# First adaLN modulation of a hybrid decoder layer: features on the partitions, one multiply-and-sum per column

## The chip, the cores and the metric

The kernel runs on one core of a Trainium2 chip. The metric is the device time of one execution in microseconds, as the median of several runs. The core has five engines with a queue each: TensorE (PE, whose weight loads are shown as PEld), VectorE (DVE), ScalarE (ACT), GpSimd (POOL) and SyncE (SP), which only issues transfers. Every queue is worked through in its own order, and semaphores tie the queues together.

## The reference, cut to what matters

One decoder layer on x of 512 tokens by 1024 features, with a conditioning vector c of 1024 numbers:

```
c_act = silu(c)
mod = c_act @ w_ada + b_ada                       # 1024 x 6144, all float32
sh1, sc1, g1, sh2, sc2, g2 = split(mod, 6)
h = rmsnorm(x, gain0) * (1 + sc1) + sh1
proj = h @ w_in                                   # queries, keys, values of both head groups
x = x + g1 * rmsnorm(attention(proj) @ w_out, gain1)
h = rmsnorm(x, gain2) * (1 + sc2) + sh2
x = x + g2 * rmsnorm(square(relu(h @ w1 + b1)) @ w2 + b2, gain3)
```

The change concerns how sh1 and sc1 (2048 of the 6144 numbers of mod) are computed, and what stands around that.

## The kernel before

Every large product is made in three float32r passes: a matrix is split into a high part (ACT, a copy) and a low part (the rest, by DVE or POOL), and the passes are high by high, high by low and low by high. Features are cut into eight chunks of 128 (KC), tokens into four tiles of 128 (NT).

The first stage goes from the start to the end of six products (q and k of three pairs of heads), which gather in six of the eight PSUM banks (qk_ps). It loops over the chunks kc. For each chunk, `w0_split` makes the high and the low part of the input weights (ACT, then two POOL instructions), `chunk_in` transposes x of this chunk on PE into a PSUM bank, applies the modulation on ACT twice (once rounded into hh, once in place) and takes the difference on DVE into hl. PE then runs 18 products of 128 by 512: six with w0hi and hh, six with w0lo and hh, six with w0hi and hl. The modulation of a chunk needs two columns for its 128 features, sh1 and sc1, with features on the partitions.

These columns are sums of 1024 terms. Before the change, a weight tile has 128 of the 1024 inputs on the partitions, and `acc0` and `ada_acc` add eight such slices, each scaled by one number of silu(c) for each partition (two on ACT, six on DVE, in two accumulators, which DVE adds). `ada_sums` then sums over the partitions on PE with a column of ones and leaves the result in PSUM, and `ada_cols` adds the bias and makes (1 + sc1) times the gain. Chunks 0 and 1 are made alone, chunks 2 to 7 in pairs (`groups`).

The order of every engine in the first stage is written out by hand (`tc.manual_schedule`): an instruction waits behind those that the program names before it on its engine. In the chunk loop the counter k tells at which of the 18 products something is issued. The sums of a pair stand in the PE queue at k = 2 of odd chunks, the transposes of the next chunk at k = 6 or 8. All large loads are issued by SP, in the order of the program; the weight tiles of the modulation rotate through 12 buffers. Nine bfloat16 products of zeros (`heat`) stand ahead of the first transposes. After the first stage, the order of ACT, DVE, POOL and SP is a planner's, which works from its own estimates, while PE's order stays written out by hand; near the end everything is by hand again.

The rows of x are normalised first: `square` on ACT gives the sums of squares into s2 (half of the last tile on DVE), `rstd` adds on DVE and takes the power on POOL, `scale_x` multiplies.

What follows the stage: `ws.make` splits three blocks of the value weights behind chunks 5, 6 and 7 (ACT, then DVE at L85); three further blocks reuse their raw buffers, and SP issues those loads, then others, then the first bias strips (L602), which are read from vec_1, a small table that the kernel computes and stores in DRAM at its start. DVE adds the strips to the scores at L649. The other four parts of mod are made later by `ada_wide` on DVE, on the way through attention.

## Time and profile before

| | us |
|---|---|
| median of 3 runs | 622.37 |
| lowest, highest | 621.87, 622.49 |
| profiled execution | 623.07 |
| its span, first to last instruction | 621.3 |
| PE busy in the span | 580.3 |
| DVE busy | 315.2 |
| ACT busy | 279.2 |
| POOL busy | 321.6 |

The span is what the trace covers; the 1.8 us between it and the execution's time lie outside of the first and the last instruction. Busy time is a sum over the span and says nothing about which engine ends last in a stretch.

### The profile page before, as it was taken

What the parts mean: (1) busy time and instruction counts of PE and PEld (TensorE: products, weight loads), DVE (VectorE), ACT (ScalarE), POOL (GpSimd) and SP (SyncE); (2) the same over time, 40 slices, a digit from 0 to 9 for tenths busy, and PEclk for the clock granted to TensorE, in tenths of its full rate; (3) what the DMA queues carried; (4) which work ended last, traced back from release to release, by engine and by line L of the source; (5) the groups of instructions that cost most, each with busy time, mean ns of one, the idle gap of its engine ahead of it and who ended that gap; (6) DMA issues with size and microseconds to landing.
All of it is one profiled execution on the core that took longest, in us unless ns stands there. A gap on an engine that the chain in (4) does not pass through costs nothing.

```text
span 621.3 us, 8137 instructions
## 1 busy us (share of the span) xinstructions
PE 580.3 (93%) x2829; PEld 482.0 (78%) x2829; DVE 315.2 (51%) x599; ACT 279.2 (45%) x532; POOL 321.6 (52%) x333
## 2 busy tenths in 40 slices
PE   2789989999897999999999999999999999999994
PEld 0477889887675888898888888788888888888883
DVE  4646679999998756535255555522401111111037
ACT  4624776578667545773233332233522333323122
POOL 1514234666898653636555555655544444446432
PEclk9969999999998999999999999999999999999998
DMA  8990569686466207734244432223232233333105
GB/s 308 419 383 1 189 129 260 128 170 224 140 185 207 84 1 270 236 106 149 89 136 136 146 125 99 80 93 101 71 112 89 100 103 102 102 101 116 56 17 186
DMA packets 29677, 89.31 MB, mean 144 GB/s; under 512 B 3427, under 2 KB 7587, under 8 KB 29636
## 3 DMA queue, kind: packets, MB, share of 16 engines
q1 hardware_dynamic: 28816, 86.52, 43.5%
q10 hardware_dynamic: 692, 2.23, 0.9%
q8 instruction: 22, 0.36, 0.3%
q14 instruction: 19, 0.16, 0.1%
q0 software_dynamic: 128, 0.05, 0.1%
HBM read 84.56 MB, written 4.22 MB: 143 GB/s over the span
## 4 chain that ended last, share of the span: by engine, by line
PE 55%; DVE 2%; ACT 2%; DMA 1%; issue 1%; POOL 0%; DVEq 0%; POOLq 0%; ACTq 0%; SPq 0%
PE u L97 9%; PE u L98 9%; PE u L96 9%; PE y L98 9%; PE y L97 9%; PE y L96 9%; DVE zg L1090 1%; ACT hf L379 1%; DMA x<-in_x 1%; ACT h2h L378 0%; DVE x L933 0%; DMA out_x<-zg 0%; ACT sq L208 0%; PE adarow L299 0%; POOL zg L1087 0%
## 5 line engine op out<-in xcount | busy, mean ns | idle before, releaser
L85 POOL TENSOR_TENSOR wlo<-raw,whi 128x512 fp32r<-128x512 f32 (+1 forms) x140 | 192.4, 1393 | 157.7 <-ACT whi L83 157.2
L83 ACT ACTIVATE whi<-raw 128x1024 fp32r<-128x1024 f32 (+5 forms) x87 | 80.7, 934 | 130.8 <-PE u L97 108.9
L97 PE MATMUL u<-h2l,whi 128*128 128x512 f32 (+1 forms) x280 | 104.2, 372 | 1.2 <-POOL h2l L380 1.1
L96 PE MATMUL u<-h2h,whi 128*128 128x512 f32 (+1 forms) x280 | 104.7, 374 | 0.0
L98 PE MATMUL u<-h2h,wlo 128*128 128x512 f32 (+1 forms) x280 | 103.8, 371 | 0.0
L97 PE MATMUL y<-wlo,ring_h2h 128*128 128x512 f32 x232 | 90.2, 389 | 0.0
L98 PE MATMUL y<-whi,ring_h2l 128*128 128x512 f32 x232 | 90.2, 389 | 0.0
L96 PE MATMUL y<-whi,ring_h2h 128*128 128x512 f32 x232 | 90.1, 389 | 0.0
L284 DVE SCALAR_TENSOR_TENSOR adaacc<-adar,c_act,adaacc 128x512 f32<-128x512 f32 x56 | 66.7, 1191 | 0.0
L97 PEld LDWEIGHTS u<-h2l,whi 128*128 128x128 f32 x280 | 52.7, 188 | 11.3 <-POOL h2l L380 1.7
L96 PEld LDWEIGHTS u<-h2h,whi 128*128 128x128 f32 x280 | 52.7, 188 | 9.2 <-ACT whi L83 0.2
L98 PEld LDWEIGHTS u<-h2h,wlo 128*128 128x128 f32 x280 | 52.7, 188 | 9.2
L663 POOL TENSOR_SCALAR w<-w,st 128x128 f32<-128x128 f32 (+2 forms) x64 | 38.2, 599 | 38.2 <-DVE st L662 32.8
L97 PEld LDWEIGHTS y<-wlo,ring_h2h 128*128 128x128 f32 x232 | 43.5, 188 | 9.1
L96 PEld LDWEIGHTS y<-whi,ring_h2h 128*128 128x128 f32 x232 | 43.5, 188 | 9.0
L98 PEld LDWEIGHTS y<-whi,ring_h2l 128*128 128x128 f32 x232 | 43.5, 188 | 9.0
L656 ACT ACTIVATE w<-w,st 128x128 f32<-128x128 f32 (+3 forms) x64 | 33.4, 522 | 28.2 <-DVE st L649 26.1
L85 POOL TENSOR_TENSOR w0lo<-w0raw,w0hi 128x384 fp32r<-128x384 f32 x16 | 17.2, 1095 | 29.3 <-ACT w0hi L83 29.3
L672 PE MATMUL p<-ident,w 128*128 128x128 f32 x136 | 25.9, 279 | 6.4 <-POOL w L663 5.9
L672 PEld LDWEIGHTS p<-ident,w 128*128 128x128 f32 x136 | 17.3, 142 | 13.4 <-POOL w L663 9.6
L686 ACT ACTIVATE pth<-p 128x384 fp32r<-128x384 f32 (+3 forms) x48 | 22.2, 466 | 10.1 <-PE p L672 9.6
L687 DVE TENSOR_TENSOR ptl<-p,pth 128x384 fp32r<-128x384 f32 (+3 forms) x48 | 25.0, 523 | 0.8 <-ACT pth L686 0.6
(222 smaller groups left out, 1093.9 us busy)
## 6 DMA issues: line engine op xcount, KB each, us to landing
raw<-in_w SPq DMA_DIRECT2D x63, 512.0 KB, 3.3
adar<-in_ada_r SPq DMA_DIRECT2D x32, 512.0 KB, 4.1
ada<-in_ada_c SPq DMA_DIRECT2D x16, 512.0 KB, 8.6
woraw<-in_w_out SPq DMA_DIRECT2D x8, 512.0 KB, 4.4
raw<-in_w_in SPq DMA_DIRECT2D x7, 512.0 KB, 6.7
w0raw<-in_w_in SPq DMA_DIRECT2D x8, 384.0 KB, 9.1
strip<-vec SPq DMA_DIRECT2D x24, 128.0 KB, 4.1
xn<-in_x SPq DMA_DIRECT2D x4, 512.0 KB, 10.0
```

What stands on the lines that cost most here:

```text
L83: nc.scalar.activation(hi[:, a:b], src[:, a:b], AF.Copy)
L85: return eng.tensor_sub(lo[:, a:b], src[:, a:b], f32(hi[:, a:b])).ins
L96: nc.tensor.matmul(ps, lh, rh, start=start, stop=False, **kw)
L97: nc.tensor.matmul(ps, lh, rl, start=False, stop=False, **kw)
L98: nc.tensor.matmul(ps, ll, rh, start=False, stop=stop, **kw)
L284: nc.vector.scalar_tensor_tensor(a, w, c_act[:, j:j + 1], a, op0=ALU.mult, op1=ALU.add)
L379: nc.scalar.activation(hf[:, :n], tp, AF.Identity, bias=sh_col, scale=a_col)
L656: anchor["act"] = nc.scalar.activation(w[:, :m], w[:, :m], AF.Exp, bias=st[:, 0:1], scale=-1.0, accum_out=st[:, 1:2]).ins
L663: nc.gpsimd.tensor_scalar(w[:, :n], w[:, :n], st[:, 2:3], 1.0, op0=ALU.mult, op1=ALU.mult)
L672: nc.tensor.transpose(p_ps[:, (c0 + j) * P:(c0 + j + 1) * P], self.w[i][:, j * P:(j + 1) * P], ident)
L686: nc.scalar.activation(dst(self.pth), src, AF.Copy)
L687: nc.vector.tensor_sub(dst(self.ptl), src, f32(dst(self.pth)))
```

## The change

Each partition now holds one output feature, and the 1024 inputs lie on the free axis: a weight tile is 128 features by 1024 inputs, two tiles (sh1, sc1) for each chunk. silu(c) is spread over all partitions once (eight products with the identity on PE, two copies on ACT into c_bc). A column is then one DVE instruction that multiplies tile and c_bc and sums along the free axis (`ada_dot`); chunk 0 is made in halves of 512. The pass over the partitions on PE, the ACT scalings and the accumulators go. Columns are made chunk by chunk, two chunks ahead of their use, and not in pairs. The input to `ada_cols` lies in SBUF (sums0) instead of PSUM. Loads follow use: chunk 0's tiles, x, then for each chunk its input weights and the next chunk's tiles. `chunk_in` is cut into `hi_in` and `lo_in`, with DVE's two sums around `lo_in`. The clearing of s2 comes after chunk 0's columns in DVE's queue, the two copies into vec_sb come behind the first `square` on ACT, the store of vec_1 goes from ACT's queue to SP's, and there are eight heat products instead of nine, in the PE queue behind the spreading of c and the two vec products, with no sums ahead of them.

```diff
-    groups = [(0,), (1,), (2, 3), (4, 5), (6, 7)]
+    ada_raws = [[] for _ in range(KC)]
+    def ada_load(kc):
+        for b in range(2):
...
-    ada_load(0, 2)
-    ada_load(1, 2)
+    ada_load(0)
     for i in range(NT):
         nc.sync.dma_start(out=xn[i], in_=x[i * P:(i + 1) * P, :])
+    for kc in range(1, KC):
+        w0_load(kc - 1)
+        ada_load(kc)
+    w0_load(KC - 1)
...
+    c_bc = first.tile([P, DM], F32, name="c_bc")
+    for h in range(2):
+        ps = bank(f"cbc{h}")
+        for j in range(4):
+            nc.tensor.matmul(ps[:, j * P:(j + 1) * P], c_act[:, 4 * h + j:4 * h + j + 1].to_broadcast([P, P]), ident,
+                             start=True, stop=True)
+        nc.scalar.activation(c_bc[:, h * 512:h * 512 + 512], ps, AF.Copy)
...
-    nc.scalar.dma_start(out=vec_1.rearrange("q h n -> h q n"), in_=vec_sb)
...
+    def ada_dot(kc, b, cs, acc):
+        junk = first.tile([P, 1024], F32, tag="dot", name=f"dot{kc}_{b}_{cs.start}", bufs=1)
+        nc.vector.scalar_tensor_tensor(junk[:, cs], ada_raws[kc][b][:, cs], 1.0, c_bc[:, cs], op0=ALU.mult,
+                                       op1=ALU.mult, accum_out=acc)
+    def dot(kc, b):
+        ada_dot(kc, b, slice(0, 1024), sums0[:, kc, b:b + 1])
+    def cols(kc):
+        ada_cols(0, [kc], sums0[:, kc, :])
...
-    pairs = [(g, next(g)) for g in (acc0(0), acc0(1))]
+    for h in range(2):
+        for b in range(2):
+            ada_dot(0, b, slice(h * 512, h * 512 + 512), parts0[:, h, b:b + 1])
+    nc.vector.tensor_add(sums0[:, 0, :], parts0[:, 0, :], parts0[:, 1, :])
+    cols(0)
     nc.vector.memset(s2[:, :, 0:2], 0.0)
     for i in range(NT):
...
         square(junk[:, :n], xn[i][:, :n], s2[:, i, 0:1])
+        if i == 0:
+            for q, ps in enumerate(vec_ps):
+                nc.scalar.activation(vec_sb[:, q, :], ps[0:8, :NVEC], AF.Copy)
+            nc.sync.dma_start(out=vec_1.rearrange("q h n -> h q n"), in_=vec_sb)
-    for j in range(9):
+    for j in range(8):
         nc.tensor.matmul(cold, heat[:, 0:P], heat, start=True, stop=True)
...
     w0_split(0)
-    chunk_in(0)
-    for i in range(NT):
-        scale_x(i, 1, act=i >= 2)
-    g = acc0(2)
-    acc = next(g)
+    hi_in(0)
+    scale_x(0, 1)
+    scale_x(1, 1)
+    scale_x(2, 1, act=True)
+    scale_x(3, 1, act=True)
+    dot(1, 0)
+    dot(1, 1)
+    lo_in(0)
+    cols(1)
...
         for k in range(18):
+            if nxt < KC and k == (8 if kc else 11):
+                hi_in(nxt)
+                if nxt + 1 < KC:
+                    dot(nxt + 1, 0)
+                lo_in(nxt)
+                if nxt + 1 < KC:
+                    dot(nxt + 1, 1)
+                    cols(nxt + 1)
```

## Rows read from the trace of the kernel before

**Rows 1.** The page: busy time of every engine over the span.
```profile
PE 580.3 (93%) x2829; PEld 482.0 (78%) x2829; DVE 315.2 (51%) x599; ACT 279.2 (45%) x532; POOL 321.6 (52%) x333
```

**Rows 2.** Windows: stretch, its length, busy time of each engine, PEclk, DMA, GB/s.
```profile
28.00:34.00 6.00, 0.85 (x5) 0.80 (x4) 5.71 (x7) 1.87 (x3) 2.71 (x3) 0.71 1.02 413
34.00:41.00 7.00, 7.00 (x23) 5.79 (x23) 2.64 (x7) 1.42 (x2) 0.00 (x0) 0.51 1.03 420
72.00:100.00 28.00, 25.29 (x172) 24.28 (x170) 23.49 (x56) 20.45 (x49) 10.40 (x14) 1.00 0.79 216
100.00:200.00 100.00, 91.41 (x514) 76.11 (x513) 96.31 (x247) 72.31 (x182) 71.49 (x97) 0.99 0.66 177
200.00:500.00 300.00, 298.79 (x1435) 249.88 (x1434) 128.88 (x177) 119.99 (x204) 160.33 (x146) 0.99 0.36 119
```

**Rows 3.** Timeline of PE at 33 us: start, duration, instruction, count, idle before.
```profile
33.23 1.84 PE L249 MATMUL adaps<-ones,acc 128*128 128x1 f32 x8 [5.15 <-DVE acc L322]
34.93 2.05 PE L436 MATMUL qk<-hh,w0hi 128*128 128x512 f32 x4
```

**Rows 4.** Timeline of DVE in the same stretch.
```profile
27.54 0.69 DVE L396 TENSOR_TENSOR hl<-tp,hh 128x512 fp32r<-128x512 f32 x1 [1.23 <-ACT tp L395]
28.15 4.21 DVE L228 SCALAR_TENSOR_TENSOR acc<-ada,c_act,acc 128x512 f32<-128x512 f32 x4
```

**Rows 5.** Timeline of PE: first products of chunks 6 and 7.
```profile
63.47 1.53 PE L436 MATMUL qk<-hh,w0hi 128*128 128x512 f32 x6
...
68.05 1.52 PE L436 MATMUL qk<-hh,w0hi 128*128 128x512 f32 x6
```

**Rows 6.** Timeline of the start, all engines, up to the first product.
```profile
3.89 0.17 DVE L204 TENSOR_TENSOR c_act<-c_sb,ce 128x8 f32<-128x8 f32 x1
...
5.59 2.72 PE L310 MATMUL vec<-oneh,rel_sb 33*8 33x384 f32 x4 [5.59 <-DMA rel_sb<-in_rel]
...
11.84 1.06 ACT L208 ACTIVATE sqx<-xn 128x1024 f32<-128x1024 f32 x1 [0.88 <-DMA xn<-in_x]
...
15.60 0.63 ACT L208 ACTIVATE sqx<-xn 128x512 f32<-128x512 f32 x1 [0.15 <-DMA xn<-in_x]
...
16.48 3.98 PE L350 MATMUL cold<-heat 128*128 128x512 bf16 x9
...
18.54 0.68 DVE L357 SCALAR_TENSOR_TENSOR sqy<-xn 128x512 f32<-128x512 f32 x1
...
19.58 0.56 POOL L213 TENSOR_TENSOR s2x<-s2x,mhalf 128x1 f32<-128x1 f32 x1 [0.76 <-DVE s2x L212]
...
20.94 0.78 ACT L394 ACTIVATE hh<-tp,mods 128x512 fp32r<-128x512 f32 x1 [3.63 <-PE tp L371]
...
21.77 1.66 PE L436 MATMUL qk<-hh,w0hi 128*128 128x512 f32 x6 [0.87 <-ACT hh L394]
```

**Rows 7.** Timeline of PE: four transposes at the low clock.
```profile
37.64 1.05 PE L371 MATMUL tp<-ident,xn 128*128 128x128 f32 x4
```

**Rows 8.** Timeline of DVE and POOL, narrow stretches where both read SBUF.
```profile
28.72 1.03 POOL L85 TENSOR_TENSOR w0lo<-w0raw,w0hi 128x384 fp32r<-128x384 f32 x1 [0.44 <-ACT w0hi L83]
28.81 1.49 DVE L228 SCALAR_TENSOR_TENSOR acc<-ada,c_act,acc 128x512 f32<-128x512 f32 x1
...
48.66 1.47 POOL L85 TENSOR_TENSOR w0lo<-w0raw,w0hi 128x384 fp32r<-128x384 f32 x1
49.18 0.15 DVE L256 TENSOR_TENSOR mods<-adaps,bada_c 128x4 f32<-128x4 f32 x1
49.37 0.21 DVE L259 TENSOR_SCALAR mods<-mods,gain_c 128x1 f32<-128x1 f32 x1
```

**Rows 9.** Timeline behind the stage: SP's issues and DVE.
```profile
72.89 0.97 SPq L602 DMA_DIRECT2D strip<-vec  x1
...
67.85 1.89 DVE L85 TENSOR_TENSOR wlo<-raw,whi 128x960 fp32r<-128x960 f32 x2 [0.23 <-ACT whi L83]
...
81.38 0.29 DVE L649 CUSTOM_DVE_ANT_0 w<-s,strip 128x128 f32<-128x128 f32 x1 [2.96 <-DMA strip<-vec]
```

More of the change, by code (lines that the diff above doesn't have):

```diff
@@ L217, in halves, with ada_sums @@
         return [t[:, 0:512], t[:, 512:1024]]
-    def ada_acc(accs, raws, per, begin):
-        n = 1024 // per
-        for b, raw in enumerate(raws):
-            for j in range(per):
-                if b * per + j >= begin:
-                    w = raw[:, j * n:(j + 1) * n]
-                    cj = c_act[:, b * per + j:b * per + j + 1]
-                    nc.vector.scalar_tensor_tensor(accs[j % 2], w, cj, accs[j % 2], op0=ALU.mult, op1=ALU.add)
-                    yield
     mods = const.tile([P, 2, KC, 3], F32, name="mods")
-    def ada_sums(layer, kcs, acc, wait=lambda: None):
+    def ada_sums(layer, kcs, acc):
         n = 2 * len(kcs)
-        if layer:
-            sums = small.tile([P, n], F32, tag=f"sums{n}", name=f"sums{layer}_{kcs[0]}")
-            for h in range(0, n, 4):
-                m = min(4, n - h)
-                ps = bank(f"adaps{layer}_{kcs[0]}_{h}")
-                for s in range(m):
-                    nc.tensor.transpose(ps[:, s * P:(s + 1) * P], acc[:, (h + s) * P:(h + s + 1) * P], ident)
-                wait()
-                nc.vector.tensor_reduce(out=sums[:, h:h + m], in_=ps[:, :m * P].rearrange("p (s q) -> p s q", q=P),
-                                        op=ALU.add, axis=mybir.AxisListType.X)
-            return sums
-        ps = bank(f"adaps{layer}_{kcs[0]}")
-        for s in range(n):
-            nc.tensor.matmul(ps[:, s:s + 1], acc[:, s * P:(s + 1) * P], ones[:, 0:1], start=True, stop=True)
-        return ps
+        sums = small.tile([P, n], F32, tag=f"sums{n}", name=f"sums{layer}_{kcs[0]}")
+        for h in range(0, n, 4):
+            m = min(4, n - h)
+            ps = bank(f"adaps{layer}_{kcs[0]}_{h}")
+            for s in range(m):
+                nc.tensor.transpose(ps[:, s * P:(s + 1) * P], acc[:, (h + s) * P:(h + s + 1) * P], ident)
+            nc.vector.tensor_reduce(out=sums[:, h:h + m], in_=ps[:, :m * P].rearrange("p (s q) -> p s q", q=P),
+                                    op=ALU.add, axis=mybir.AxisListType.X)
+        return sums
     def ada_cols(layer, kcs, ps):
@@ L395, in chunk_in, with lo_in @@
         nc.scalar.activation(tp, tp, AF.Identity, bias=sh_col, scale=a_col)
-        nc.vector.tensor_sub(hl[:, kc, :], tp, f32(hh[:, kc, :]))
+    def lo_in(kc):
+        nc.vector.tensor_sub(hl[:, kc, :], tps[kc], f32(hh[:, kc, :]))
+    tps = {}
     w0_split(0)
-    chunk_in(0)
-    for i in range(NT):
-        scale_x(i, 1, act=i >= 2)
-    g = acc0(2)
-    acc = next(g)
-    def some(n):
-        for _ in range(n):
-            next(g, None)
+    hi_in(0)
[7 more added lines that the diff above has]
+    cols(1)
     for kc in range(KC):
@@ L1125, in _lay_out @@
     unit = lambda m: m.transpose(1, 0, 2).reshape(P, -1)
[L1126 removed]
+    wt = a["w_ada"][0].reshape(DM, 2, 3, KC, P)[:, 0, 0:2]
+    o["ada_c"] = c(wt.transpose(3, 2, 1, 0).reshape(P, KC * 2 * DM))
     o["ada_r"] = c(np.stack([unit(m) for m in (w[:, :, 0, 2], cols(1, range(4)), cols(1, range(4, 8)), w[:, :, 1, 2])]))
```

66 lines of the change are left out of this document (9 added, 57 removed).

## The prediction

> **What bounds the kernel now.** The page comes first. PE is busy for 580.3 of 621.3 us [rows 1], so whatever shortens the run must take idle time, or slow time, out of PE's queue. The windows say where that time lies. From 200 to 500 us PE idles 1.2 us in all, and nothing can be won there [rows 2]. From 72 to 200 us DVE is the fuller engine (23.5 of 28 us, then 96.3 of 100) and PE idles 2.7 and 8.6 us. From 28 to 34 us PE works 0.85 of 6 us; from 34 to 41 us it is busy all the time, but at a granted clock of 0.51, the lower of its two levels (1.2 instead of 2.4 GHz).
>
> The timeline explains the hole. PE waits 5.15 us, until 33.23, for the accumulator of chunks 2 and 3 [rows 3]. DVE is late with it: after the hl of chunk 1 at 27.54 come four scaled sums, which take 4.21 us, and the addition [rows 4]. The partition sums of that pair stand in PE's queue ahead of 16 products of chunk 1. After the idle stretch the clock is low, and it is back at full level by 41 [rows 2]. So the first stage is set by DVE's queue, and then by the clock.
>
> What a chunk costs when nothing is late: from the first product of chunk 6 to that of chunk 7 it is 68.05 - 63.47 = 4.58 us, 18 products and four transposes [rows 5], so about 0.222 us for a product and 0.56 us for the transposes. The first product starts at 21.77 [rows 6]. Eight such chunks, the last without transposes, would be 36.1 us and end at 57.9. The stage ends at 72.2 (68.05 plus 18 products and the last one's tail). Some 14 us are there to be won, and not more.
>
> **The start.** Before, the chain is x, squares, power, scaling, transposes, hh, first product. The first square waits for x until 11.84, the last until 15.60 [rows 6]. Two of the eight 512 KB loads ahead of the end of x now come later: at the 413 GB/s of this stretch [rows 2] that is 1.05 MB or 2.5 us, so x lands from about 9.3 to 13.1. But the clearing of s2 now stands behind chunk 0's columns on DVE, and the squares write into s2. How late is that?
>
> silu(c) is ready at 4.06 [rows 6], and I let PE begin at 4.2. The eight spreading products are two passes each, as two vec products show as x4 [rows 6]. Each pass loads 128 columns and streams 128. No row has this form. The nearest is a float32 transpose at the low clock: 1.05 / 4 = 0.26 us [rows 7]. The bound above is load and stream one after the other: 0.26 plus what 128 of vec's 384 columns take (2.72 / 4 / 3 = 0.23 [rows 6]), 0.49. I take 0.26, as the same load and stream stand in that row: 16 passes are 4.2 us, the two halves end at 6.3 and 8.4, and ACT copies them in some 0.6 each. DVE's four halves are of the form of L357, 0.68 us for 512 columns with the sum [rows 6], 0.72 with the hand-over: 7.0 to 8.4 and 9.1 to 10.5. Additions and clearing end at 11.05. The squares then run 11.1 to 16.6, with vec_sb's two copies (about 0.5 each) among them, against 11.84 to 16.3 before. The earlier x is thus mostly given away. The last power comes at 17.2, not 19.58, since DVE's half square and additions stand free now; scaling, transposes, and hh (0.78) put the first product at 19.2, 2.6 us earlier. With serial passes it would be 22.9.
>
> **The clock at the start.** The heat products lie behind vec and need nothing else, so PE runs them at about 11 to 13.4 and then has four transposes until 19.2. Before, they ran from 16.48, right up to the transposes [rows 6]. An idle stretch like this one cost the high level at 31 us, and it came back some 6 us after the products began at 34.93 [rows 2, 3]. I take the same here: products at twice 0.222 for 6 us, a loss of 3.0 us (bounds: 0 if the level holds, 3.0 or more otherwise). Chunk 0 then ends at 26.9.
>
> **The chunks.** PE loses the partition sums and ACT the scalings; neither was last at full pace, so I count nothing for them beyond the waits. DVE's work for a chunk: two sums over 1024. From 256 to 512 columns such an instruction grows by 0.0010 us a column as the rows of L228 have it (0.74 for 512), so 0.68 + 0.53 = 1.21, 1.24 with the hand-over. With hl (0.66 to the next) and the two small ones (0.15 and 0.21 [rows 8]) that is 3.5 us, below PE's 4.58. But POOL makes w0lo, twice 1.0 us a chunk, and the two engines take turns: DVE's sum begun at 28.81 takes 1.49 instead of 0.74, as POOL works until 29.7 [rows 8]. 3.5 + 2.0 is 5.5 at worst, 3.5 at best.
>
> The Trainium skill, "SBUF — State Buffer", section "SBUF: two separate sides", says why: VectorE with two SBUF inputs and GpSimd hold a shared port pair in turn, each for its whole instruction. Rows 8 agree. The same rule speaks against a detail of this change: L256 read its sums from PSUM and took 0.15 us during a POOL instruction that had 48.66 to 50.13 [rows 8]; now both its inputs lie in SBUF, and it would wait. By the rule the stage ends at 61.4, without it for L256 at 58.2.
>
> What decides is a loop that closes once a chunk. hh needs the columns, the second ACT pass follows hh, hl follows that, on DVE the second sum of the next-but-one chunk stands behind hl, and the columns behind that: 0.75 + 0.68 + 0.66 + 1.24 + 0.37 and four hand-overs of 0.05 are 3.9 us. If L256 waits for one POOL instruction of 1.0, it is 4.9; when another falls before the sum, 5.9. I laid out the queues of PE, ACT, DVE and POOL by these durations: chunks 1 and 2 go at PE's pace (end 36.0), chunks 3 to 7 take 4.7 to 5.9, 5.1 on the mean: 36.0 + 25.4 = 61.4. I take the waiting L256, since other two-input sums wait. That is 10.8 us before 72.2.
>
> Weights of the modulation are not late: chunk 7's land after some 13 MB, 13 / 0.413 = 32 us and the start, near 37, and are used at 52. Their buffers are freed by chunk 1's sums at 22.4, before SP comes to them.
>
> **Behind the stage.** Not all 10.8 us arrive. The third value block's split (DVE, L85) ended at 69.74, 2.5 us before the stage; in my layout DVE's queue puts it behind the last columns and hl, at 61.5. SP's third reload waits for it, the strips queue behind, and the first bias sum waited 2.96 us for its strip until 81.38 [rows 9], ahead of a stretch in which DVE is the bound. That start moves by 69.74 - 61.5 = 8.2 us. I count 8.5, a little PE gain included. vec_1's store costs SP one issue, hidden by strips that are read 40 us later. 623.07 - 8.5 = 614.6 for the profiled execution, 0.7 above the median, so 613.9.
>
> **Rivals.** (a) As worked out: 612 to 617, chance 0.52. (b) L256 doesn't wait and PE sets the pace: the stage ends at 58.2, the splits 12 us earlier: 610.4. For it: DVE has 1 us of slack a chunk; against: rows 8. 0.18. (c) The spreading passes are serial: first product at 22.9, 3.7 us later, stage end at 65.1, 3.7 us less gain: 617.6. 0.12. (d) The other side: the clock stays low. A chunk at the low level is 18 x 0.444 + 4 x 0.26 = 9.0 us, 4.4 more than 4.58. Low through chunk 3 it takes back what was won; low for 40 us, the stage ends at 74.8 and the run at 625. For it: the long gap ahead of the first product; against: from 34.93 on it rose under the same kind of products [rows 2, 3]. 0.05. (e) The change gives nothing: the long sum costs 2.2 us instead of 1.24, DVE needs 6.9 us a chunk, the stage ends at 72.1: 622. Against: L357 is the same form. 0.05. (f) The planner lays the order from 72 to 200 us otherwise. DVE has under 9 us of slack in 128, so some us go either way; only a loss of 8.5 would turn the sign. 0.08.
>
> **How the numbers follow.** The forecast is (a). 608.5 to 620 takes in (b), (c), and most of (f), and leaves out (d), (e) and the far ends, under 0.2. Differences below 0.2% (1.2 us) can't be told from no change. Faster: (a), (b), (c), most of (f) and a little of (e), 0.89. Same: rest of (e) and some of (f), 0.03. Slower: (d) and the remainder, 0.08.
>
> **What would show it.** First product near 19 us; clock at 0.5 in its first 6 us; no PE idle above 2 us from there on; hh waiting for L259 from chunk 3; L256 near 1 us after the second sum's end in chunks with POOL at work; last product of the stage near 61; first L649 near 73. The prediction is wrong if the stage ends above 66, or if it ends near 61 and the first 100:200 DVE stretch eats the gain.

## The result, and the profile after

| | before | after |
|---|---|---|
| median, same chip (us) | 622.12 | 608.24 |
| lowest, highest | 621.68, 622.49 | 607.16, 608.40 |
| ratio of the times, 95% interval | | 0.9773, [0.9756, 0.9790] |
| profiled execution, its span | 623.07, 621.3 | 608.38, 606.6 |

The change makes the kernel 13.9 us faster. The forecast was 613.9, with a range down to 608.5: the sign was right, the gain was larger than forecast, and the time lies 0.3 us below the range. One execution of the first experiment, in which every product ran at half pace, is left out of its times.

The page of the kernel after, busy time of each engine [rows 1]:

```profile
PE 573.3 (95%) x2812; PEld 478.0 (79%) x2812; DVE 322.0 (53%) x604; ACT 274.5 (45%) x524; POOL 327.1 (54%) x333
```

DVE and POOL are busy for longer than before. PE is busy for 7.0 us less and idle for 7.7 us less (33.3 instead of 41.0), with almost as many instructions: the kernel won less by doing less work than by losing less time, in waits and at the low clock. The windows of the kernel after, same stretches and columns as [rows 2]:

```profile
28.00:34.00 6.00, 6.00 (x30) 4.92 (x29) 5.93 (x9) 3.36 (x5) 3.67 (x3) 1.00 1.03 404
34.00:41.00 7.00, 7.00 (x36) 5.77 (x35) 6.93 (x12) 3.34 (x5) 4.12 (x3) 1.00 1.03 409
72.00:100.00 28.00, 26.35 (x172) 24.49 (x173) 27.87 (x80) 21.35 (x60) 13.87 (x18) 1.00 0.79 179
100.00:200.00 100.00, 90.72 (x503) 75.21 (x502) 93.47 (x242) 68.88 (x170) 76.01 (x109) 0.98 0.62 175
200.00:500.00 300.00, 298.77 (x1420) 249.39 (x1419) 119.29 (x145) 116.17 (x190) 158.48 (x132) 1.00 0.34 117
```

The hole of 28 to 34 us is gone, and with it the low clock of 34 to 41 (1.00, was 0.51). What is new is DVE's column: 5.93 of 6 and 6.93 of 7 us, with PE full as well. The two engines run level, and neither has slack.

The start, from the timelines of PE, DVE and ACT of the kernel after [rows 6]:

```profile
4.37 3.76 PE L284 MATMUL cbc<-ident,c_act 128*128 128x128 f32 x16 [4.37 <-DVE c_act L197]
...
10.81 0.07 DVE L326 MEMSET s2x<- 128x8 f32 x1
...
10.91 1.06 ACT L201 ACTIVATE sqx<-xn 128x1024 f32<-128x1024 f32 x1 [2.16 <-DVE s2x L326]
...
9.52 1.90 PE L336 MATMUL cold<-heat 128*128 128x512 bf16 x8
18.66 2.92 PE L411 MATMUL qk<-hh,w0hi 128*128 128x512 f32 x6 [0.87 <-ACT hh L378]
```

The first square waits 2.16 us for the clearing of s2, as forecast. The first six products take 2.92 us, against 1.52 at full pace. The granted clock says so too; windows of the kernel after:

```profile
16.00:18.00 2.00, 0.95 (x2) 0.36 (x2) 1.46 (x6) 0.68 (x2) 1.62 (x3) 0.50 1.04 412
...
20.00:22.00 2.00, 2.00 (x6) 1.51 (x6) 1.97 (x3) 1.86 (x3) 0.06 (x1) 0.52 1.04 414
22.00:24.00 2.00, 2.00 (x13) 1.66 (x12) 1.96 (x6) 0.43 (x1) 2.00 (x2) 1.00 1.03 408
```

The chunks, from PE's timeline of the kernel after (first products of chunks 1, 2, 6 and 7 [rows 5]):

```profile
24.84 1.53 PE L411 MATMUL qk<-hh,w0hi 128*128 128x512 f32 x6
29.43 1.52 PE L411 MATMUL qk<-hh,w0hi 128*128 128x512 f32 x6
...
47.76 1.66 PE L411 MATMUL qk<-hh,w0hi 128*128 128x512 f32 x6
54.23 1.65 PE L411 MATMUL qk<-hh,w0hi 128*128 128x512 f32 x6 [1.62 <-ACT hh L378]
```

Chunks 1 to 5 take 4.54 to 4.66 us each, PE's own pace. Only chunk 7 starts late, by one hole of 1.62 us, and the next timeline, DVE's, shows where it comes from: two instructions of the wide modulation (L257, L259), placed there by the planner, stand ahead of chunk 7's column addition (L231).

```profile
48.55 0.48 DVE L257 TENSOR_SCALAR adaacc<-adar,c_act 128x512 f32<-128x512 f32 x1
48.95 0.68 DVE L382 TENSOR_TENSOR hl<-tp,hh 128x512 fp32r<-128x512 f32 x1
49.55 1.21 DVE L302 SCALAR_TENSOR_TENSOR dot<-ada,c_bc 128x1024 f32<-128x1024 f32 x1
...
50.69 1.49 DVE L259 SCALAR_TENSOR_TENSOR adaacc<-adar,c_act,adaacc 128x512 f32<-128x512 f32 x1
52.11 0.95 DVE L231 TENSOR_TENSOR mods<-sums,bada_c 128x2 f32<-128x2 f32 x1
```

One ordinary cycle on DVE, earlier in the same timeline [rows 4, 8]:

```profile
29.85 0.68 DVE L382 TENSOR_TENSOR hl<-tp,hh 128x512 fp32r<-128x512 f32 x1
30.45 1.21 DVE L302 SCALAR_TENSOR_TENSOR dot<-ada,c_bc 128x1024 f32<-128x1024 f32 x1
...
31.71 0.85 DVE L231 TENSOR_TENSOR mods<-sums,bada_c 128x2 f32<-128x2 f32 x1
...
32.72 1.88 DVE L302 SCALAR_TENSOR_TENSOR dot<-ada,c_bc 128x1024 f32<-128x1024 f32 x1
...
34.53 0.68 DVE L382 TENSOR_TENSOR hl<-tp,hh 128x512 fp32r<-128x512 f32 x1
```

From hl (29.85) to hl (34.53) it is 4.68 us, without idle time: 0.1 us more than PE's 4.57. DVE falls behind by that much a chunk, and chunk 5 is the first that takes longer on PE, 4.66.

Behind the stage, from the timelines of DVE and SP [rows 9]: the third split ends at 57.68, the strip is issued at 61.54, and the first bias sum starts at 68.74.

```profile
55.78 1.90 DVE L85 TENSOR_TENSOR wlo<-raw,whi 128x960 fp32r<-128x960 f32 x2 [0.23 <-ACT whi L83]
...
61.54 0.46 SPq L577 DMA_DIRECT2D strip<-vec  x1
...
65.82 0.69 DVE L503 SCALAR_TENSOR_TENSOR q<-qk,q 64x512 fp32r<-64x512 f32 x1 [0.62 <-ACT q L502]
68.74 0.29 DVE L624 CUSTOM_DVE_ANT_0 w<-s,strip 128x128 f32<-128x128 f32 x1 [2.22 <-PE s L617]
```

The releaser in the last row is to be doubted: that score product had begun at 65.54 and takes 0.28 us. The engine that it names had long been done.

Seven marks, read from the timelines of either kernel (us; a chunk's or a stretch's first instruction, but the split's end):

```
                         before   after   earlier by
first product             21.77   18.66     3.11
stage end (first v)       72.12   58.45    13.67
third split, end          69.74   57.68    12.06
first bias sum            81.38   68.74    12.64
first out-projection y   189.61  175.81    13.80
first u                  256.83  242.16    14.67
end of span              621.3   606.6     14.7
```

By PE's timelines, the 13.67 us at the stage's end come from these places. The first product gives 3.11. Chunk 1, with the hole and most of the low clock behind it, gives 9.82 (14.41 us before, 4.59 after). Chunks 3 and 5, in which the sums of the other two pairs stood, give 3.25 together (6.24 and 6.23 before, 4.56 and 4.66 after). Chunk 0 takes back 0.49 (5.69 before, 6.18 after), and chunk 6 with the hole behind it 1.89 (4.58 before, 6.47 after).

### The profile page after: what moved, and what is told of

It is laid out like the page before. It is cut to its first block, busy times and chain, and to the rows that moved or that the text cites. A ratio compares the mean times of both kernels' runs of the same rounds, so it can differ in the third digit from the quotient of the medians.

```text
span 606.6 us, 8099 instructions
## 1 busy us (share of the span) xinstructions
PE 573.3 (95%) x2812; PEld 478.0 (79%) x2812; DVE 322.0 (53%) x604; ACT 274.5 (45%) x524; POOL 327.1 (54%) x333
## 4 chain that ended last, share of the span: by engine, by line
PE 56%; DVE 2%; ACT 2%; DMA 1%; issue 1%; POOL 0%; DVEq 0%; POOLq 0%; ACTq 0%; SPq 0%
PE u L97 10%; PE u L98 9%; PE u L96 9%; PE y L97 9%; PE y L98 9%; PE y L96 9%; DVE zg L1065 1%; DMA x<-in_x 1%; ACT hf L363 1%; ACT h2h L362 0%; DVE x L908 0%; DMA out_x<-zg 0%; ACT sq L201 0%; PE adarow L274 0%; POOL zg L1062 0%
## 5 line engine op out<-in xcount | busy, mean ns | idle before, releaser
L259 DVE SCALAR_TENSOR_TENSOR adaacc<-adar,c_act,adaacc 128x512 f32<-128x512 f32 x56 | 65.8, 1175 | 0.0
L85 POOL TENSOR_TENSOR w0lo<-w0raw,w0hi 128x384 fp32r<-128x384 f32 x16 | 22.1, 1402 | 13.8 <-ACT w0hi L83 13.8
L1002 DVE TENSOR_TENSOR ring_h2l<-rsq_hl,ring_h2h 128x512 fp32r<-128x512 f32 x8 | 5.5, 694 | 38.0 <-ACT ring_h2h L1001 38.0
```

Source lines behind the costliest of these rows:

```text
L85: return eng.tensor_sub(lo[:, a:b], src[:, a:b], f32(hi[:, a:b])).ins
L259: nc.vector.scalar_tensor_tensor(a, w, c_act[:, j:j + 1], a, op0=ALU.mult, op1=ALU.add)
```

## The experiments

Their order is that in which they were run; a table of their marks stands at the end. Each edit is against the kernel after, if nothing else is said.

**The clearing of s2 ahead of chunk 0's columns.**

```diff
+    nc.vector.memset(s2[:, :, 0:2], 0.0)
     for h in range(2):
         for b in range(2):
             ada_dot(0, b, slice(h * 512, h * 512 + 512), parts0[:, h, b:b + 1])
...
-    nc.vector.memset(s2[:, :, 0:2], 0.0)
```

> Only the clearing of s2 moves ahead of chunk 0's sums in DVE's queue. In the changed kernel the first square idles 2.16 us until that clearing, at 10.91. If the clearing is what the start waits for, the first square begins near 9.2 (x landed, ACT's second copy into c_bc done at 8.8), the first product near 17.0 instead of 18.66, and the run gains 1.5 to 2 us. If x's landing or the copies of vec_sb set the start, nothing moves (under 0.5 us).

606.36 us, ratio 0.9746 [0.9720, 0.9773]. The time alone does not separate it from the kernel after, whose interval overlaps. The start does, read in the run further below that has this edit and one more: there the first square starts at 9.10 instead of 10.91, waiting for x and no longer for the clearing, and the first product at 16.84 instead of 18.66. It is the clearing that does it: with the other edit alone the first square still waits for the clearing, until 11.02, and the first product comes at 18.76.

**Zero products that keep the clock.** Twenty at the start instead of eight, and fourteen between and behind the first four transposes.

```diff
-    for j in range(8):
+    for j in range(20):
         nc.tensor.matmul(cold, heat[:, 0:P], heat, start=True, stop=True)
...
+            for j in range(warm[i]):    # (4, 4, 2, 4) in chunk 0
+                nc.tensor.matmul(qk_ps[0], heat[:, 0:P], heat, start=True, stop=True)
```

> Heat products go from 8 to 20 behind vec, and 4, 4, 2, 4 more behind the four first transposes, so that PE works up to the first product. In the changed kernel the granted clock falls at 15 and the first six products take 0.44 us each. If the idle stretch from 11.4 to 14.3 is the cause, the clock stays at the high level through 22 us, the first six products take 0.22, and chunk 0 goes from 6.2 to about 4.9 us; gain 1.3 us of stage. The rival is that chunk 1's columns (ready at 23.4) hold chunk 1 anyway: then PE waits for hh of chunk 1 and the gain is under 0.5.

609.70 us, ratio 0.9799 [0.9768, 0.9830]: nothing won. PE's timeline of this kernel, chunk 0:

```profile
18.27 1.66 PE L413 MATMUL qk<-hh,w0hi 128*128 128x512 f32 x6
...
22.78 1.66 PE L413 MATMUL qk<-hl,w0hi 128*128 128x512 f32 x6 [1.02 <-DVE hl L384]
```

The six products take 1.66 instead of 2.92 us: the clock was kept. But then PE waits 1.02 us for hl, which stands behind chunk 1's column sums in DVE's queue (it starts at 22.04), and the next chunk starts only 0.57 us earlier than in the kernel after. Full clock moves the wait to DVE.

**The wide modulation not before the last split**, so that it cannot stand ahead of chunk 7's columns.

```diff
+    anchor["dve"] = ws.last_lo
```

> The planner's two early adaacc instructions (0.48 and 1.49 us, in DVE's queue ahead of chunk 7's columns in the changed kernel) are kept behind the last instruction of the stage; nothing else is asked for, but the planner's order behind the stage may differ. If they make the 1.6 us hole of PE ahead of chunk 7, the hole goes and the stage ends near 56.8 instead of 58.5; the run gains 1 to 2 us unless the order behind the stage takes it back. If the hole comes from POOL's turn alone it stays above 1 us.

608.52 us, ratio 0.9772 [0.9742, 0.9802]: no change in the time. The hole is gone (chunk 7 starts at 52.38, the stage ends at 56.58, 1.87 us earlier), which shows the cause of the hole; but the first out-projection product comes at 176.17, 0.36 later than in the kernel after. The first bias sum comes 1.33 us earlier, and the stretch from there to the out-projection takes 1.69 us longer, with the planner's order on DVE changed (see the next section). What the rest of the loss is, no run shows.

**A column addition with one input from SBUF.**

```diff
-        nc.vector.tensor_add(m[:, :, 0:2], ps[:, 0:2 * n].rearrange("p (k s) -> p k s", s=2),
-                             bada_c[:, layer, kcs[0]:kcs[0] + n, :])
+            for s in range(2):
+                nc.vector.tensor_scalar(m[:, 0, s:s + 1], ps[:, s:s + 1], bada_c[:, 0, kcs[0], s:s + 1], 1.0,
+                                        op0=ALU.add, op1=ALU.mult)
```

> The addition of L231 (0.85 us in the changed kernel, two SBUF inputs) becomes two one-input instructions with the bias as a per-partition scalar. By the prediction's layout the wait of this addition is worth 3 us of the stage. By the trace of the changed kernel PE already sets the pace (4.57 us a chunk, against 4.58 at best), so the columns come 0.4 to 0.6 us earlier, the next sum waits that much longer for POOL instead, and the stage gains under 0.5 us.

607.38 us, ratio 0.9765 [0.9738, 0.9792]. DVE's timeline of this kernel:

```profile
30.95 0.33 DVE L233 TENSOR_SCALAR mods<-sums,bada_c 128x1 f32<-128x1 f32 x2
...
31.44 1.53 DVE L307 SCALAR_TENSOR_TENSOR dot<-ada,c_bc 128x1024 f32<-128x1024 f32 x1
```

Two instructions that read one SBUF tensor and a pointer take 0.33 us where one that read two took 0.85: the addition had waited for POOL. DVE now has slack, chunks 1 to 6 go at 4.55 to 4.56 us, chunk 7 starts at 52.12 without a hole and the stage ends at 56.20. The two adaacc instructions still stand ahead of chunk 7's last columns in DVE's queue, and the chunks in between are hardly faster. So the waiting addition had its part in the hole (which takes both it and the adaacc instructions) and hardly any in the pace.

**Chunk 1's weight tiles ahead of x again.**

```diff
     ada_load(0)
+    ada_load(1)
     for i in range(NT):
         nc.sync.dma_start(out=xn[i], in_=x[i * P:(i + 1) * P, :])
     for kc in range(1, KC):
         w0_load(kc - 1)
-        ada_load(kc)
+        if kc > 1:
+            ada_load(kc)
```

> The changed kernel with chunk 1's weight tiles loaded ahead of x again, as before the change. If the load order matters only through x at the start, x lands 2.5 us later, the first square starts near 11.8 instead of 10.9, and the run loses 0.5 to 1.5 us. If the order of loads is a main part of the gain, 4 us or more are lost.

610.63 us, ratio 0.9824 [0.9782, 0.9867]. The first square starts at 11.51 instead of 10.91, the first product at 19.26 (0.60 later), the stage ends at 59.07 (0.62 later). The new order of the loads is worth about 0.6 us where it acts, since in the kernel after the squares wait for the clearing anyway; the time does not tell the two apart, as the intervals overlap.

**Half as long sums for chunks 2 to 7.** The columns of these chunks are sums over 512 of the 1024 inputs; the rest is left out.

```diff
-        ada_dot(kc, b, slice(0, 1024), sums0[:, kc, b:b + 1])
+        ada_dot(kc, b, slice(0, 1024 if kc < 2 else 512), sums0[:, kc, b:b + 1])
```

> The sums of chunks 2 to 7 run over 512 of the 1024 inputs (the other half is left out), 1.1 us less DVE work a chunk. If PE sets the pace of the chunks already, chunks 1 to 5 stay at 4.57 us, only the hole ahead of chunk 7 shrinks, and the run gains 0.5 to 2 us. If DVE's loop sets the pace as the prediction had it, the stage gains 0.5 us or more in each of chunks 3 to 7 beyond that, 3 us in all.

605.21 us, ratio 0.9732 [0.9684, 0.9780]. With half the work in the sums the chunks still take 4.55 us each: PE sets the pace. The stage ends at 55.82, 2.63 us earlier, of which 1.62 is the hole.

**One more sum a chunk** (512 columns, its result unused).

```diff
                 if nxt + 1 < KC:
                     dot(nxt + 1, 1)
+                    ada_dot(nxt + 1, 1, slice(0, 512), parts0[:, 0, 0:1])
```

> For each of chunks 2 to 7 one more sum over 512 columns (0.7 us, its result unused) stands in DVE's queue behind the second sum. In the changed kernel DVE works 6.93 of 7 us in the stage and needs about 4.67 us a chunk. If DVE is level with PE, a chunk now takes 5.3 us or a little more, the stage ends 4 to 5 us later and the run loses 3 to 5. If DVE had the slack of 1 us a chunk that the plain durations give, under 1 us is lost.

617.29 us, ratio 0.9927 [0.9904, 0.9951]. The timelines of PE and DVE of this kernel:

```profile
30.56 1.64 PE L412 MATMUL qk<-hh,w0hi 128*128 128x512 f32 x6 [0.58 <-ACT hh L378]
...
36.49 1.65 PE L412 MATMUL qk<-hh,w0hi 128*128 128x512 f32 x6 [1.11 <-ACT hh L378]
...
37.12 0.69 DVE L382 TENSOR_TENSOR hl<-tp,hh 128x512 fp32r<-128x512 f32 x1 [0.41 <-ACT tp L379]
...
38.98 1.38 DVE L302 SCALAR_TENSOR_TENSOR dot<-ada,c_bc 128x512 f32<-128x512 f32 x1
```

From here a chunk takes 5.93 us (36.49 - 30.56), 1.36 more than in the kernel after, the stage ends 6.5 us later and the run loses 9, more than the 4 to 5 and 3 to 5 expected. The sum of 0.69 us takes 1.38 beside POOL, and DVE now idles 0.41 us a cycle for ACT's second pass, which itself waits for the columns: the loop of the prediction closes. More work on DVE costs at once, and more than its own duration; less work gains nothing in the pace. So DVE stood at the edge.

**The kernel before, with its sums later in PE's queue.** In chunk 1 the partition sums stand at k = 14 and the transposes at k = 16 instead of 2 and 8.

```diff
-                if k == 2:
+                if k == (14 if kc == 1 else 2):
...
-                elif k == 8:
+                elif k == (16 if kc == 1 else 8):
```

> The kernel before, with only the place of the partition sums of chunks 2 and 3 in PE's queue moved from the third to the fifteenth product of chunk 1 (and the transposes of chunk 2 from the ninth to the seventeenth). If the 5.15 us wait there and the low clock after it are the main part of the 14 us, PE works on until about 31, the clock stays at the high level, and the run gains 5 to 7 us. If DVE's lateness is only met again at chunk 2, it gains under 2 us.

619.58 us, ratio to the kernel before 0.9972 [0.9948, 0.9995]. PE's timeline of this kernel, the sums of the three pairs [rows 3] and the first products of chunk 2:

```profile
33.18 1.02 PE L249 MATMUL adaps<-ones,acc 128*128 128x1 f32 x8 [2.46 <-DVE acc L322]
...
36.08 2.77 PE L436 MATMUL qk<-hh,w0hi 128*128 128x512 f32 x6
...
43.00 1.02 PE L249 MATMUL adaps<-ones,acc 128*128 128x1 f32 x8 [0.49 <-DVE acc L322]
...
54.33 1.02 PE L249 MATMUL adaps<-ones,acc 128*128 128x1 f32 x8 [1.03 <-DVE acc L322]
```

DVE's accumulator comes as late as before. PE does other work in the meantime, but still waits 2.46 us instead of 5.15, and the clock falls behind that wait too: six products take 2.77 us. The second pair waits as before (0.49, was 0.51), the third longer (1.03, was 0.52), again with the low clock behind it (0.50 from 56 to 58 us). This placing gives 2.5 us of span, where 5 to 7 were expected; whether another would give more was not tried.

**No low splits for chunks 2 to 7**, so that POOL does not work beside DVE.

```diff
+        if kc < 2:
             split_to(*w0[kc], w0_raw[kc])
+        else:
+            w0[kc][1] = w0[0][1]
+            nc.scalar.activation(w0[kc][0], w0_raw[kc], AF.Copy)
```

> The low parts of the input weights are made for chunks 0 and 1 only; chunks 2 to 7 use chunk 0's low part again (this leaves out twelve POOL instructions of 1.0 us, so q and k lack their right low parts). Nothing else changes. Theory 1 (from chunk 2 on, DVE's column sums of 1.87 us and the column addition of 0.85 us hold 0.66 and 0.69 us of waiting for POOL; DVE's cycle of 4.67 us stands level with PE's 4.57): the first sum of a chunk falls to about 1.21 us, the addition to 0.16 to 0.2, DVE's share of 34 to 41 us from 99% to about 70%, the chunks stay at 4.55 us because PE sets them, and the hole of 1.62 us ahead of chunk 7 goes or shrinks below 0.4; the stage ends near 56.2 instead of 58.45, the run is 1 to 2 us faster than 608.2. Rival (the prediction's picture, in which POOL costs DVE so much that DVE sets the pace): chunks fall by 0.5 us each, the stage ends near 55 or below. Rival (POOL plays no part; 1.87 is what such a sum costs when the array of TensorE is at work): sums stay at 1.87, nothing changes.

606.23 us, ratio 0.9746 [0.9706, 0.9786]. DVE's timeline of this kernel:

```profile
34.42 1.22 DVE L302 SCALAR_TENSOR_TENSOR dot<-ada,c_bc 128x1024 f32<-128x1024 f32 x1
...
35.68 0.16 DVE L231 TENSOR_TENSOR mods<-sums,bada_c 128x2 f32<-128x2 f32 x1
...
38.36 0.69 DVE L387 TENSOR_TENSOR hl<-tp,hh 128x512 fp32r<-128x512 f32 x1 [1.13 <-ACT tp L384]
```

1.88 and 0.85 us fall to 1.22 and 0.16: 1.35 us of every cycle on DVE was waiting for POOL. DVE is now idle 1.13 us a cycle, and the chunks take 4.55 to 4.57 as before. The hole is gone, the stage ends 1.7 us earlier.

**The clearing and the one-input addition together.**

> Two edits together: s2 is cleared before chunk 0's columns (alone 606.4), and the column addition takes the bias as a pointer, one input from SBUF (alone 607.4). If they act in different places, the first at the start and the second at the hole ahead of chunk 7, they add up: first product near 17.7, stage end near 55.2 instead of 58.45, the run near 605.5 (604.5 to 606.5). Rival (what is won in the first stage is met again by DVE between the first score and the out-projection): 606.4 to 607.5, no better than either alone.

604.45 us, ratio 0.9718 [0.9683, 0.9753]; stage end 55.40. In the stage they add up (0.86 us up to chunk 1, and the 2.25 of the addition alone; 3.05 together), as they act in different places; the time lies below the rival's, but its interval overlaps those of either edit alone. The first product comes 1.82 us earlier (16.84), but the clock is still low until 22 us, chunk 0 takes 7.14 us instead of 6.18, and chunk 1 starts only 0.86 us earlier.

**With the zero products as well.**

> The kernel of the run before plus the zero products of the warm start (20 instead of 8, and fourteen between the transposes of chunk 0), which alone kept the clock but gave 609.7. Theory (in that run the gain was met by DVE's queue, whose column sums of chunks 1 and 2 were not ready): the clock stays at its upper level, PE waits about 1 us for the hl of chunk 0 and again until the sums are through, chunk 1 starts at most 0.6 us earlier than without the zero products, the stage ends within 0.5 us of it, and the time is within 1 us of it. Rival (the low clock was the only loss there): chunk 1 starts 1.5 us earlier and the run is 1.5 us faster.

605.63 us, ratio 0.9756 [0.9713, 0.9798]. Chunk 1 starts at 22.35, 1.63 us before that of the run above, and the stage ends 1.64 us earlier: the rival was right on the stage, the theory wrong. The theory had left out that the earlier clearing brings DVE's queue forward as well: hl of chunk 0 starts at 20.12, was 22.04 with the zero products alone, and PE does not wait for it. Yet the time is not better. DVE's timeline of this kernel:

```profile
64.38 0.29 DVE L631 CUSTOM_DVE_ANT_0 w<-s,strip 128x128 f32<-128x128 f32 x1 [3.86 <-DMA strip<-vec]
```

The first bias sum came 0.75 us earlier only, after 3.86 us of waiting for its strip. That raises the question whether the strip was last in the kernel after, too.

**The first head's strip read early**, in the kernel after, behind chunk 4 (and two buffers for the others instead of three).

```diff
+            if h < 1:
+                t = keep.tile([P, 512], F32, tag=f"strip{h}", name=f"strip{h}")
...
+        if kc == 4:
+            strip_of(0)
```

> The changed kernel with one bias strip moved: the strip of the first head is read behind chunk 4 of the first stage instead of behind the value weights that wait for the third split (and two buffers for the other strips instead of three). In the changed kernel the first bias sum starts at 68.74 although its scores are there at 65.82; its strip is issued at 61.54. Theory (the strip, and with it the end of the third split, is what the first bias sum waits for, as before the change): the first bias sum starts near 66.3, 2.4 us earlier; with DVE the fuller engine up to 185 us the first out-projection product comes up to 2 us earlier than 175.8, the run is 0.5 to 2 us faster than 608.2. Rival (it is the chain from the scores that sets it, the strip lands in time): the sum stays at 68.5 to 68.8, the run unchanged. Rival (the sum comes earlier, but DVE's work up to 185 us, and not its start, is met by another wait): sum near 66.3, out-projection and run unchanged.

607.23 us, ratio 0.9771 [0.9756, 0.9787]. DVE's timeline of this kernel:

```profile
65.70 0.29 DVE L630 CUSTOM_DVE_ANT_0 w<-s,strip 128x128 f32<-128x128 f32 x1 [0.78 <-PE s L623]
```

The bias sum starts 3.04 us earlier, right behind its scores: in the kernel after it was the strip that came last, not the score product that the row named. Some 0.8 us of the 3.04 are, by an estimate, DVE's order: the instruction of 65.82, which ends at 66.51 in the kernel after, stands behind the bias sum here, at 66.70. The out-projection follows 1.89 us earlier, the span ends 1.0 us earlier; in the median that is within what can be told apart.

**All edits, with the strip on SP.**

> The kernel with the earlier clearing, the one-input column addition and the zero products (605.6, stage end 53.6, first bias sum 64.38 after 3.86 us of waiting for its strip), with the first head's strip read behind chunk 4. Theory (the stage's gain stops at the strip): the first bias sum comes near 61.4, 3 us earlier, the first out-projection product near 170 instead of 172.6, the run 603 to 604.5. Rival (behind the stage DVE's queue is as full as it can be in the planner's order, and the strip only moves the idle time): the bias sum near 61.5, the out-projection at 172 to 173, the run 605 to 606.5.

605.68 us, ratio 0.9765 [0.9743, 0.9786]: no better than without the strip's edit. DVE's timeline of this kernel:

```profile
51.72 0.78 DVE L262 TENSOR_SCALAR adaacc<-adar,c_act 128x512 f32<-128x512 f32 x1 [2.70 <-DMA adar<-in_ada_r]
```

The strip held SP until the table that it reads had landed (issued at 39.51, the table's store at 31.56). The loads behind it came some 7 us later, and DVE waited 2.70 us for one, which makes a hole of 1.25 us on PE. The stage ended at 57.79, 4.03 us later than without the strip's edit; 2.78 of that were there at the first product already (20.11), as the zero products ahead of it ran at a slower pace (last section), long before the strip was issued. Nothing follows on the question.

**The same strip issued by ACT behind chunk 5**, first without and then with the zero products.

```diff
+            eng = nc.sync if h else nc.scalar
-            nc.sync.dma_start(out=t[:, 256:], in_=bass.AP(tensor=vec_1.tensor, offset=row, ap=[[1, P], [1, 256]]))
+            eng.dma_start(out=t[:, 256:], in_=bass.AP(tensor=vec_1.tensor, offset=row, ap=[[1, P], [1, 256]]))
...
-        if kc == 4:
+        if kc == 5:
             strip_of(0)
```

> The kernel with the earlier clearing and the one-input column addition (604.5, first bias sum 65.13 after 1.95 us of waiting for its strip, its scores done at 62.8), with the first head's strip read behind chunk 5 and issued by ACT, so that SP's queue, where the run before made the value weights 7 us late, is as it was. Theory (the strip sets the first bias sum, the sum sets the stretch behind it): first bias sum near 63.0 to 63.5, first out-projection product near 170.5 instead of 172.3, the run 603 to 604. Rival (only the place of the idle time changes, DVE's work up to 185 us is the bound in whatever order): sum near 63.3, out-projection 172 to 172.5, the run 604 to 605.

602.40 us, ratio 0.9678 [0.9645, 0.9712]. That is below the kernel after, whose interval it does not touch, and the lowest median of all, 19.7 us below the kernel before. From the same kernel without the strip's edit (604.45) it is not told apart, as the intervals overlap. The bias sum starts at 63.29, 1.84 us earlier than without this edit, the out-projection at 171.57, 0.70 earlier; the profiled execution (604.99) is the longest of six, and by u nothing is left in it of the gain (next section).

> The kernel with the zero products as well (605.6, stage end 53.6, first bias sum 64.38 after 3.86 us of waiting for its strip, its scores done at 61.1), with the first head's strip read behind chunk 5 and issued by ACT. Theory: first bias sum near 61.4 to 62, first out-projection product near 169.5 to 170.5 instead of 172.6, the run 602.5 to 604. Rival (DVE's work up to 185 us is the bound in whatever order): sum near 61.5, out-projection 172 to 173, the run 605 to 606.

603.67 us, ratio 0.9698 [0.9666, 0.9731], not told apart from the run above. Bias sum 62.26, out-projection 170.45, 2.2 us before that of the same kernel with the late strip, whose bias sum was 2.1 us later. Theory, in the trace: the start of the bias sums sets the stretch behind it. In the times the two kernels are not told apart, as the intervals overlap.

The marks of all runs but the first (profiled executions, us):

```
                      first    stage   split   bias    out-            span
                      product  end     end     sum     proj.   u       end
kernel after          18.66    58.45   57.68   68.74   175.81  242.16  606.6
zero products         18.27    58.23   57.43   68.91   176.04  243.42  607.3
wide part later       18.58    56.58   55.81   67.41   176.17  242.31  606.8
one-input addition    18.76    56.20   55.41   66.30   173.41  240.76  604.6
old load order        19.26    59.07   58.30   69.76   176.93  243.09  607.6
half sums             18.43    55.82   53.91   65.72   172.78  240.27  604.1
one more sum          18.73    64.97   64.19   76.22   184.53  251.97  616.4
before, sums later    21.68    69.64   67.27   78.69   186.91  254.39  618.8
no low splits         18.59    56.75   54.97   66.72   173.78  240.09  604.6
clearing + addition   16.84    55.40   54.18   65.13   172.27  238.59  603.1
  + zero products     17.33    53.76   52.96   64.38   172.64  238.80  603.3
strip early (SP)      18.58    58.29   57.50   65.70   173.92  241.12  605.6
all, strip on SP      20.11    57.79   57.00   65.20   173.46  238.69  602.5
cl. + add. + strip    17.10    55.88   54.66   63.29   171.57  238.80  603.2
  + zero products     17.44    54.86   54.08   62.26   170.45  237.71  602.1
```

## Why the prediction was too careful

Forecast for the profiled execution: 8.5 us less. Measured: 14.7. What bounded the kernel was seen rightly. What failed is the size of four terms: the low clock at the start (3.0 us put, 1.6 measured), POOL's turns in the chunk loop (two of 1.0 us put, 1.35 in all measured, so that a chunk kept PE's pace), the place of the third split (0.1 us behind the stage put, 0.77 ahead measured), and the gain behind the first bias sum (0.3 us put, without a working, 2.06 measured). All four err to the same side. Term by term, in the prediction's own steps:

| step | forecast | measured | difference |
|---|---|---|---|
| first product | 19.2 | 18.66 | 0.5 |
| chunk 0, with the low clock | 7.7 | 6.18 | 1.5 |
| chunks 1 and 2 | 9.1 | 9.13 | 0.0 |
| chunks 3 to 7 | 25.4 | 24.48 | 0.9 |
| third split's end against the stage's | 0.1 behind | 0.77 ahead | 0.9 |
| from the split to the first bias sum | 11.64 as before | 11.06 | 0.6 |
| gain behind the first bias sum | 0.3 | 2.06 | 1.8 |
| sum | 8.5 | 14.7 | 6.2 |

**Right.** What bounded the stage: with DVE's pair sums out of PE's queue, the hole and the low clock behind it are gone. That the clearing of s2 holds the squares until about 11 us, so that the earlier x is mostly given away. That the column addition, now with two inputs from SBUF, waits for POOL: 0.85 instead of 0.15 us [rows 8]. The run without the low splits and the one with the one-input addition show it from both sides. The Trainium skill, "SBUF — State Buffer", section "SBUF: two separate sides", says that VectorE with two SBUF inputs and GpSimd hold a shared port pair in turn; the trace agrees, 1.88 us for a sum beside POOL and 1.22 without it. That the third split, through SP's queue, sets the first bias sum: in the twelve kernels without an early strip, the two before among them, the sum starts 10.9 to 12.0 us behind the split's end, from 64.4 to 81.4 us; with the strip early it comes right behind its scores.

**Wrong: the low clock at the start.** It was to cost 3.0 us, 6 us at half pace. It cost 1.6 (6.18 against 4.58): the first product came at 18.66, the granted clock was up from 22. The run with the earlier clearing shows that the size hangs on the start: with the first product at 16.84 the clock was low until 22 as well, and chunk 0 took 7.14. Nor was all of the 1.6 there to be had: with the clock kept chunk 0 still took 6.00 (the run with the zero products alone), as PE then waited for hl. Windows of the run with the earlier clearing and the one-input addition:

```profile
20.00:22.00 2.00, 2.00 (x7) 1.50 (x6) 1.97 (x7) 0.05 (x1) 1.88 (x2) 0.50 1.03 411
22.00:24.00 2.00, 2.00 (x12) 1.71 (x11) 1.44 (x2) 1.42 (x2) 0.34 (x1) 0.95 1.02 404
```

The 6 us were taken over from another place of the trace, behind the hole [rows 2, 3], and the delay is no constant: here the clock was back at about 22 us whether the products had begun at 18.66 or at 16.84.

**Wrong: the pace of chunks 3 to 7.** The forecast has it that "chunks 3 to 7 take 4.7 to 5.9, 5.1 on the mean". The four full chunks of them took 4.56, 4.57, 4.66 and, with the hole, 6.47, so that the sum of 24.48 is near the forecast's 25.4 in part by luck: without the unforeseen hole it would be some 1.9 less. The forecast added a whole POOL instruction twice in a cycle; the trace has 1.35 us of waiting a cycle (0.66 at the sum, 0.69 at the addition), and DVE's cycle of 4.68 us is only 0.1 above PE's pace. That the loop was rightly drawn and only its length was off, the run with one more sum shows: there DVE idles for ACT within the loop, and a chunk takes 5.93 us. The hole ahead of chunk 7 was not foreseen: not the loop, but two instructions of the wide modulation that the planner put into DVE's queue.

**Wrong: what is behind the stage.** The mechanism held, the place did not: DVE's queue had the third split ahead of the stage's end, not behind it, 0.9 us in all. With the earlier stage end and 0.6 us less from split to sum the first bias sum came 12.64 us earlier, not 8.2. From there on, 0.3 us was forecast, and 2.06 came: 1.16 us up to the out-projection, 0.87 from there to u and 0.03 behind u.

Two regularities in the marks say what these are. From the first bias sum to the first out-projection product it is either 107.1 to 107.2 us (seven kernels, the one after among them) or 108.2 to 108.3 (eight, with the one before), and 108.8 in the one with the wide part moved behind. The two lengths go with DVE's order, which is the planner's here: in the seven, the last of the four instructions q<-qk stands ahead of the first bias sum, as in the kernel after (65.82, above), in the other nine behind it, as in the kernel before:

```profile
82.38 0.69 DVE L528 SCALAR_TENSOR_TENSOR q<-qk,q 64x512 fp32r<-64x512 f32 x1
```

So the 1.16 us go with an order that does this work in DVE's wait for the strip; no run moved that instruction alone. With the same order the stretch keeps its length to 0.1 us (but for the run with the wide part later), and its start decides: of the two kernels with zero products and both other edits, the one whose strip is issued by ACT has its bias sum 2.12 us earlier and its out-projection 2.19. In the kernels without the zero products that strip changed the order too, and of 1.84 us 0.70 were left.

From the out-projection to u the time goes with a dip of the clock, which falls behind PE's idle time there. Windows of the kernel before, of the kernel after, of the fastest version, and of the run with all edits and the strip on SP, in this order (columns as in [rows 2]):

```profile
190.00:200.00 10.00, 7.06 (x32) 4.70 (x31) 8.59 (x22) 7.55 (x15) 7.94 (x11) 0.89 0.59 188
200.00:210.00 10.00, 10.00 (x53) 8.70 (x52) 6.68 (x23) 3.90 (x12) 6.95 (x14) 0.77 0.62 184
```

```profile
180.00:190.00 10.00, 7.39 (x34) 5.75 (x33) 7.42 (x19) 5.77 (x13) 10.00 (x13) 0.83 0.73 219
```

```profile
180.00:190.00 10.00, 9.33 (x45) 7.69 (x44) 6.26 (x18) 4.16 (x11) 8.09 (x15) 0.66 0.69 223
```

```profile
180.00:190.00 10.00, 7.75 (x49) 6.40 (x48) 8.24 (x24) 5.97 (x15) 10.00 (x17) 1.00 0.66 217
```

With no dip (1.00) the stretch takes 65.2 us, with one of 0.83 it takes 66.1 to 66.4 (six kernels), with one of 0.66 it takes 67.2 to 67.5 (four); the kernel before, with 0.89 and 0.77, took 67.2, and the four others, whose dip lies across two stretches too, 67.3 to 67.5. So 0.87 of the gain goes with a shorter dip, and the fastest version has the longer one again. No run changed the dip by itself; that it is the cause is read from these rows, not shown. It need not be the change's doing: the kernel after itself ran between 607.16 us at a mean granted clock of 0.995 and 608.40 at 0.989. Behind u every kernel takes 363.8 to 364.5 us.

**The rivals.** The second (PE sets the pace, stage end at 58.2, 610.4) named the pace and the stage's end (58.45), but for a wrong reason, and so by luck: the addition does wait. The serial spreading passes are refuted: 16 passes took 3.76 us, 0.235 each. The clock that stays low, the long sum of 2.2 us (1.22 alone) and a loss from the planner's order did not come.

## What to carry to other kernels

Where two engines run level, work taken off the second one gains nothing in the pace, and work added to it costs at once (here 1.36 us a chunk for a sum of 0.69): take both engines' cycle from the trace with the waits in it, and count a shared wait by its measured length. What a stage gains reaches the end only through the next thing that starts the following stretch; here it was a small load behind a split and a full queue. Moving that load brought the bias sum forward by 1.8 to 3.0 us, though in the times no pair of kernels shows it by itself. A mark compares two kernels only if the same work stands ahead of it in both: here 1.16 us of the gain went with one instruction that DVE did ahead of the mark, in its wait, instead of behind it. A row's releaser that had ended long before names the wrong one: look for a transfer.

## What the runs showed of the hardware that was not expected

The store of the small table (24 KB), issued while loads ran at 400 GB/s, took about 8 us until a load that reads it could be issued (31.56 to 39.51 in the run with all edits and the strip on SP, 30.67 to 38.85 in the one before it). From 38 to 40 us the loads had all but ended, with 23 and 24 GB/s. The zero products at the start take 0.24 us each in the kernel after (eight in 1.90 us from 9.52), but 0.30 in the mean in the run with all edits and the strip on SP (20 in 6.01 us from 10.63), where the granted clock is shown as 1.00 from 10 to 20 us; the row of the clock does not explain that difference. Up to 13.60 us they came 0.43 us apart there, from then on 0.21.
